# Moving the two halves of x by 192 bytes and the weight units by 256 in SBUF, in a two-layer hybrid trunk on one core

## The chip, the cores and the metric

The kernel runs on one core of a Trainium2 chip. The metric is device time in microseconds (us) for one execution of the whole program; lower is better. The core has TensorE (PE in the profile, its weight loads PEld), VectorE (DVE), ScalarE (ACT), GpSimd (POOL) and SyncE (SP), which here only issues DMAs.

## The reference

Two layers, each of three residual blocks with a LayerNorm behind each: a SwiGLU block, a mixer, a second SwiGLU block. x is 512 tokens by 1024 features in float32; the inner width of a SwiGLU block is 2816.

```python
for l in range(DEPTH):                       # DEPTH = 2
    x = layer_norm(ALPHA * x + 0.5 * swiglu_ffn(x, ffn1_w_gu[l], ffn1_w_down[l]), ...)
    x = layer_norm(ALPHA * x + hybrid_mixer(x, w_in[l], w_out[l], ...), ...)
    x = layer_norm(ALPHA * x + 0.5 * swiglu_ffn(x, ffn2_w_gu[l], ffn2_w_down[l]), ...)

def swiglu_ffn(x, w_gu, w_down):
    a, u = jnp.split(x @ w_gu, 2, axis=-1)
    return (jax.nn.silu(a) * u) @ w_down
```

The mixer projects x once, runs windowed softmax attention on one group of heads and chunked retention on the other, and projects the two outputs back.

## The kernel before, in words

**Every product in three.** A float32 operand is split into a high part, rounded to the matmul format fp32r, and a low part, the rest. `split` (L168, L169) does it: ACT casts the high part, DVE subtracts it for the low one. `mm3` (L183 to L185) then issues three matmuls for one product: high by high, the stationary high with the moving low, the stationary low with the moving high. Its argument `a` is the stationary operand, loaded into the array by a weight load ahead of the matmul; `b` is the moving operand. In the profile's rows a matmul stands as `ps<-moving,stationary`: `ps<-xh,uh` streams xh past the weights uh.

**The tiles that matter here.** `xh` and `xl` are the high and low parts of the transposed x, 8 blocks of 128 features by 512 tokens, 16384 bytes a partition each. Weights arrive by DMA in `raw`, are split into `uh` and `ul` ("units", 4096 bytes a partition, six buffers each), and are handed out by `Weights.get`. `Th` and `Tl` are the split differences of x's quarters, made once in each SwiGLU block by `sums_of_x`.

**A SwiGLU block**, of which there are four. The gate and up products come in 11 steps of 256 columns; steps 2 to 10 are done by `glu7`, a seven-product scheme on 2 by 2 blocks. There the units are stationary and 256 tokens are streamed; of its 14 products of 12 matmuls, 6 stream a quarter of x (`xb`) and 8 stream a difference (`tb`). Steps 0 and 1 use `projs`, with 256 or 512 tokens of x streamed. The down projection that follows (`seventh`, `down`) turns the roles round: a slice of x's buffers, which by then hold splits of the inner activations, is stationary, and a unit is streamed, 512 columns wide. The residual, LayerNorm (`norm`) and the transposes back into xh and xl close the block.

**The mixer** streams x past stationary units for queries and keys (`emit_T`, 256 tokens wide for five of the units, and `projs`, 512 wide), and streams units past stationary x for values, gates and the output (`proj_tok`, `half`).

**Order.** The recording layer keeps the program order on TensorE and for the splits (`keep_in_program_order`); a pool's buffer is reused when its last reader is done. Pools are laid out in SBUF one behind the other in the order in which they are opened: `base`, `rawp`, `unit`, `small`, then the pools of the stage.

**Where the tiles lie.** From the built program, in bytes from the start of each partition: 2048 of DMA scratch, four constants of 32 each, `ident` (512), `mhalf` (32), and then xh at 2720, which is 160 modulo 256. xl, Y and raw follow in multiples of 256, so the units begin at 68256, also 160 modulo 256, with all twelve buffers alike. `small` takes 960 bytes, and the pools of a SwiGLU block begin at 118368. Th lies at 179808 and Tl at 196192, both 96 modulo 256. Each block and slice of these tiles that a matmul reads starts a multiple of 512 bytes behind its tile's start, so the remainder modulo 256 is the same for all of a tile's matmuls.

Of the kernel before, what the change touches and what calls it, by code (L numbers as in the profile page):

```python
# [7 lines left out]
F32 = mybir.dt.float32  # L8
# [10 lines left out]
P = 128  # L19
# [27 lines left out]
class Weights:  # L47


    def __init__(self, T, items):  # L50
        self.T, self.items = T, items
        self.emitted = self.taken = self.out = 0
        self.ready = []
        self.raws = {}
        self.last = {raw: i for i, (raw, _, _, _) in enumerate(items)}
# [44 lines left out]
class Trunk:  # L100
    def __init__(self, tc, ctx):
        self.tc, self.nc = tc, tc.nc
        self.n = 0
        self.now = 0
        self.pin = True
        self.tasks = []
        self.later = []
        self.pace = None
        self.halves = 2
        nc = self.nc  # L110
        self.base = ctx.enter_context(tc.tile_pool(name="base", bufs=1))
        self.rawp = ctx.enter_context(tc.tile_pool(name="rawp", bufs=2))
        self.unit = ctx.enter_context(tc.tile_pool(name="unit", bufs=UBUFS))
        self.small = ctx.enter_context(tc.tile_pool(name="small", bufs=3))
        self.psum = ctx.enter_context(tc.tile_pool(name="psum", bufs=8, space=PSUM))
        self.ident = self.base.tile([P, P], F32, name="ident")
        make_identity(nc, self.ident)
        self.mhalf = self.base.tile([P, 8], F32, name="mhalf")
        nc.vector.memset(self.mhalf, -0.5)
        self.xh = self.base.tile([P, KC, SEQ], F32R, name="xh")  # L120
        self.xl = self.base.tile([P, KC, SEQ], F32R, name="xl")
        self.Y = self.base.tile([P, NT, D], F32, name="Y")
# [370 lines left out]
    def norm(self, t, halves, gb, out=None, delay=4, scale=(ALPHA, ALPHA)):  # L493
        nc = self.nc
        g, b = gb
        y = self.Y[:, t, :]
        st = self.small.tile([P, 2, 6], F32, tag="st", name=self.nm("st"))
        for h in range(2):
            hs = slice(h * 512, (h + 1) * 512)
            nc.vector.scalar_tensor_tensor(out=y[:, hs], in0=y[:, hs], scalar=scale[h], in1=halves[h],  # L500
                                           op0=ALU.mult, op1=ALU.add)
            nc.vector.bn_stats(out=st[:, h, :], in_=y[:, hs])
        mv = self.small.tile([P, 2], F32, tag="mv", name=self.nm("mv"))
        nc.vector.bn_aggr(out=mv, in_=st)
        ve = self.small.tile([P, 1], F32, tag="ve", name=self.nm("ve"))
        nc.vector.tensor_scalar_add(ve, mv[:, 1:2], LN_EPS)
        rs = self.small.tile([P, 1], F32, tag="rs", name=self.nm("rs"))
        nc.gpsimd.tensor_tensor(out=rs, in0=ve, in1=self.mhalf[:, 0:1], op=ALU.pow)
        nc.vector.scalar_tensor_tensor(out=y, in0=y, scalar=mv[:, 0:1], in1=g, op0=ALU.subtract, op1=ALU.mult)
        parts = [slice(0, D)] if out is None else [slice(0, 512), slice(512, D)]  # L510
        for hs in parts:
            nc.vector.scalar_tensor_tensor(out=y[:, hs], in0=y[:, hs], scalar=rs, in1=b[:, hs],
                                           op0=ALU.mult, op1=ALU.add)
            if out is not None:
                nc.sync.dma_start(out[t * P : (t + 1) * P, hs], y[:, hs])
        if out is None:
            self.pend.append(self.spawn(self.y_to_xT(t), delay))
# [670 lines left out]
```

## Time and profile before

| | |
|---|---|
| Median of 3 runs | 1766.88 us (1766.7 to 1767.4) |
| Span of the profiled execution, first to last instruction | 1765.1 us |
| Median less that span | 1.8 us |
| TensorE busy | 99% of the span, 11930 matmuls |
| Weight loads busy | 91%, 11930 loads |
| DVE / ACT / POOL busy | 80% / 53% / 10% |

The page gives the span of the profiled execution; that execution's own device time is not listed apart, so the 1.8 us between span and median stand for what lies around the span. Matmuls overlap in the array, so the sum of their durations is more than the span; what one matmul costs when they stand in a row is the distance from its start to the next one's start, called its pitch below. "Granted clock" is the share of TensorE's clock that the throttle let through.

### The profile page before, as it was taken

The numbers are of one execution on the slowest core, as the hardware profiler recorded it, in microseconds if no ns is written. First come the engines' busy times: TensorE is split into PE (matmuls) and PEld (weight loads), VectorE is DVE, ScalarE is ACT, GpSimd is POOL, SyncE is SP. The second block draws the span as 40 slices with busy tenths as digits, with TensorE's granted clock in tenths as the row PEclk, the third lists the DMA queues.
The fourth block names the chain that finished last, engine by engine and source line by source line (L and its number), as shares of the span: only waits on it lengthen the run. The fifth ranks groups of instructions, "written<-read, shape, count | busy, mean of one in ns | idle before, by whom it ended". The sixth has DMA issues, their size and how long they took to land.

```text
span 1765.1 us, 29166 instructions
## 1 busy us (share of the span) xinstructions
PE 1752.7 (99%) x11930; PEld 1600.5 (91%) x11930; DVE 1414.9 (80%) x1975; ACT 928.1 (53%) x1456; POOL 182.9 (10%) x152
## 2 busy tenths in 40 slices
PE   9999999999999999999999999999999999999998
PEld 9999988887789999998899999889877899999886
DVE  7888888856767888878888888888567587888887
ACT  5455556378712455555535555554795234555561
POOL 0000022111111000014000000311011110000131
PEclk9999999999999999999999999999999999999999
DMA  6234389422222243369423334982233122334891
GB/s 191 97 96 133 131 202 199 131 85 88 73 79 72 74 137 102 97 208 214 140 68 99 121 96 147 211 203 91 85 95 96 48 95 97 97 96 132 211 218 48
DMA packets 163765, 216.34 MB, mean 123 GB/s; under 512 B 5168, under 2 KB 116528, under 8 KB 163632
## 3 DMA queue, kind: packets, MB, share of 16 engines
q1 hardware_dynamic: 141872, 172.55, 30.5%
q0 software_dynamic: 21760, 41.95, 13.1%
q8 instruction: 93, 1.52, 0.3%
q14 instruction: 40, 0.33, 0.1%
HBM read 212.38 MB, written 2.10 MB: 122 GB/s over the span
## 4 chain that ended last, share of the span: by engine, by line
PE 90%; issue 6%; DMA 1%; DVE 1%; POOL 1%; ACT 0%; SPq 0%; POOLq 0%; DVEq 0%
PE ps L183 29%; PE ps L185 29%; PE ps L184 29%; PE ps L476 1%; DMA raw<-in_ffn_w_gu_dram 1%; POOL sw L959 1%; PE ps L1067 1%; PE ps L1015 0%; PE ps L1029 0%; PE ps L1063 0%; PE ps L1050 0%; DMA retS<-c_retS_dram 0%; ACT sw L957 0%; DVE ul L169 0%; PE ps L1007 0%
## 5 line engine op out<-in xcount | busy, mean ns | idle before, releaser
L183 PE MATMUL ps<-xh,uh 128*128 128x256 f32 (+1 forms) x1616 | 482.2, 298 | 0.0
L185 PE MATMUL ps<-xh,ul 128*128 128x256 f32 (+1 forms) x1616 | 479.3, 297 | 1.0 <-DVE ul L169 0.9
L184 PE MATMUL ps<-xl,uh 128*128 128x256 f32 (+1 forms) x1616 | 478.5, 296 | 0.3 <-DVE xl L169 0.3
L168 ACT CAST uh<-raw 128x1024 fp32r<-128x1024 f32 (+1 forms) x274 | 237.1, 886 | 245.6 <-PE ps L184 140.1
L169 DVE TENSOR_TENSOR ul<-raw,uh 128x1024 fp32r<-128x1024 f32 (+1 forms) x274 | 273.3, 1013 | 62.2 <-ACT uh L168 61.6
L183 PE MATMUL ps<-Th,uh 128*128 128x256 f32 x1152 | 319.1, 277 | 0.0
L184 PE MATMUL ps<-Tl,uh 128*128 128x256 f32 x1152 | 318.7, 277 | 0.0
L185 PE MATMUL ps<-Th,ul 128*128 128x256 f32 x1152 | 318.3, 276 | 0.0
L185 PEld LDWEIGHTS ps<-xh,ul 128*128 128x128 f32 x1616 | 307.9, 191 | 10.1 <-DVE ul L169 1.6
L183 PEld LDWEIGHTS ps<-xh,uh 128*128 128x128 f32 x1616 | 307.9, 191 | 9.7 <-issue 1.6
L184 PEld LDWEIGHTS ps<-xl,uh 128*128 128x128 f32 x1616 | 308.0, 191 | 7.9 <-DVE xl L169 0.5
L183 PE MATMUL ps<-uh,xh 128*128 128x512 f32 x720 | 283.4, 394 | 0.5 <-ACT xh L168 0.5
L185 PE MATMUL ps<-uh,xl 128*128 128x512 f32 x720 | 280.8, 390 | 0.0
L184 PE MATMUL ps<-ul,xh 128*128 128x512 f32 x720 | 280.3, 389 | 0.0
L168 ACT CAST uh<-S 128x1024 fp32r<-128x1024 f32 x144 | 151.1, 1049 | 149.0 <-PE ps L184 145.2
L169 DVE TENSOR_TENSOR ul<-S,uh 128x1024 fp32r<-128x1024 f32 x144 | 175.9, 1222 | 60.1 <-ACT uh L168 59.5
L184 PEld LDWEIGHTS ps<-Tl,uh 128*128 128x128 f32 x1152 | 216.7, 188 | 0.0
L183 PEld LDWEIGHTS ps<-Th,uh 128*128 128x128 f32 x1152 | 216.6, 188 | 0.0
L185 PEld LDWEIGHTS ps<-Th,ul 128*128 128x128 f32 x1152 | 216.4, 188 | 0.0
L389 POOL DMA_DIRECT2D R<-in_ffn_w_down_dram x80 | 97.1, 1217 | 1020.7 <-DVE ul L169 930.0
L169 DVE TENSOR_TENSOR ul<-R,uh 128x1024 fp32r<-128x1024 f32 x120 | 145.1, 1221 | 25.8 <-ACT uh L168 25.7
L183 PEld LDWEIGHTS ps<-uh,xh 128*128 128x128 f32 x720 | 135.2, 188 | 30.1 <-issue 1.6
(143 smaller groups left out, 2362.4 us busy)
## 6 DMA issues: line engine op xcount, KB each, us to landing
raw<-in_ffn_w_gu_dram SPq DMA_DIRECT2D x86, 1024.0 KB, 5.5
R<-in_ffn_w_down_dram POOLq DMA_DIRECT2D x80, 512.0 KB, 7.6
raw<-in_w_in_dram SPq DMA_DIRECT2D x18, 1024.0 KB, 5.2
R<-in_ffn_w_down_dram SPq DMA_DIRECT2D x16, 1024.0 KB, 6.3
raw<-in_ffn_w_down_dram SPq DMA_DIRECT2D x12, 1024.0 KB, 7.2
R<-in_ffn_w_down_dram SPq DMA_DIRECT2D x8, 512.0 KB, 4.3
raw<-in_w_in_dram SPq DMA_DIRECT2D x8, 512.0 KB, 6.1
raw<-in_w_out_dram SPq DMA_DIRECT2D x8, 512.0 KB, 6.4
```

What stands on the lines that cost most here:

```text
L168: a = self.nc.scalar.copy(hi, src)
L169: b = self.low = self.nc.vector.tensor_sub(lo, src, hi.bitcast(F32))
L183: keep(mm(out, ah, bh, start=start, stop=False, **kw))
L184: keep(mm(out, ah, bl, start=False, stop=False, **kw))
L185: keep(mm(out, al, bh, start=False, stop=stop, **kw))
L389: self.nc.gpsimd.dma_start(src, rows(i, j, g * 2, 2), accum_op=ALU.add))
L476: nc.tensor.transpose(b[:, c * P : (c + 1) * P], src[:, c * P : (c + 1) * P], self.ident)
L959: nc.gpsimd.tensor_mul(sw[:, :n], sw[:, :n], S)
L1067: ins = nc.tensor.matmul(ob[:, o0 : o0 + HD], ST[h][:, n, :], vr[:, n, p * P + h * HD : p * P + (h + 1) * HD], start=n == 0, stop=n == 0 o ...
```

## The change

It moves tiles in SBUF. Three statistics tiles of 64 bytes (`st0` to `st2`) are allocated in `base` ahead of xh, in place of the rotating `st` of `small`; that moves xh, xl, Y and raw up by 192 bytes. A new pool `near` of 64 bytes stands between raw and the units, which moves the units up by 256. `ve` becomes a third column of `mv`, and a pad of 32 bytes (`behind`) is put into `small`; `small` is 256 bytes shorter by all this, so every pool behind it stays where it was. The two pads are written once, by two GpSimd memsets.

| tile | before | modulo 256 | after | modulo 256 |
|---|---|---|---|---|
| xh | 2720 | 160 | 2912 | 96 |
| xl | 19104 | 160 | 19296 | 96 |
| raw, first of two | 51872 | 160 | 52064 | 96 |
| uh, first of six | 68256 | 160 | 68512 | 160 |
| ul, first of six | 92832 | 160 | 93088 | 160 |
| Th | 179808 | 96 | 179808 | 96 |
| Tl | 196192 | 96 | 196192 | 96 |

```diff
         self.rawp = ctx.enter_context(tc.tile_pool(name="rawp", bufs=2))
+        self.near = ctx.enter_context(tc.tile_pool(name="near", bufs=1))
+        nc.gpsimd.memset(self.near.tile([P, 16], F32, name="apart"), 0.0)
         self.unit = ctx.enter_context(tc.tile_pool(name="unit", bufs=UBUFS))
...
+        nc.gpsimd.memset(self.small.tile([P, 8], F32, tag="behind", name="behind", bufs=1), 0.0)
...
+        self.stats = [self.base.tile([P, 2, 8], F32, name=f"st{i}") for i in range(3)]
+        self.norms = 0
         self.xh = self.base.tile([P, KC, SEQ], F32R, name="xh")
...
-        st = self.small.tile([P, 2, 6], F32, tag="st", name=self.nm("st"))
+        st = self.stats[self.norms % 3][:, :, :6]
+        self.norms += 1
...
-        mv = self.small.tile([P, 2], F32, tag="mv", name=self.nm("mv"))
-        nc.vector.bn_aggr(out=mv, in_=st)
-        ve = self.small.tile([P, 1], F32, tag="ve", name=self.nm("ve"))
+        mv = self.small.tile([P, 3], F32, tag="mv", name=self.nm("mv"))
+        ve = mv[:, 2:3]
+        nc.vector.bn_aggr(out=mv[:, :2], in_=st)
```

The order of instructions on TensorE, ACT, DVE and SP is what it was, with the same waits between the same instructions. On GpSimd two memsets are added at the start of the program. Its first rows before (`ident` is the identity matrix that TensorE's first matmuls use):

```order
L1174 MEMSET const-uint8-127 128x1
L1184 UNCONDITIONAL_BRANCH
masks.py:197 MEMSET ident 128x128
masks.py:199 ISA
masks.py:199 AFFINE_SELECT ident<-ident 128x128
```

And now:

```order
L1180 MEMSET const-uint8-127 128x1
L1190 UNCONDITIONAL_BRANCH
L114 MEMSET apart 128x16
L118 MEMSET behind 128x8
masks.py:197 MEMSET ident 128x128
masks.py:199 ISA
masks.py:199 AFFINE_SELECT ident<-ident 128x128
```

The two memsets stand ahead of the two instructions that make `ident`; nothing else has moved.

## The prediction

> **What bounds the kernel now.** I read the page's busy times and clock first, then the waits of TensorE, then the groups of instructions kept apart by shape, and last the order of time inside two stages.
>
> ```profile
> PE 1752.7 (99%) x11930; PEld 1600.5 (91%) x11930; DVE 1414.9 (80%) x1975; ACT 928.1 (53%) x1456; POOL 182.9 (10%) x152
> PEclk9999999999999999999999999999999999999999
> PE 90%; issue 6%; DMA 1%; DVE 1%; POOL 1%; ACT 0%; SPq 0%; POOLq 0%; DVEq 0%
> PE ps L468 <- POOL ident masks.py:199: 1.4, 1, 1.4
> PE ps L185 <- DVE ul L169: 0.9, 2, 0.7
> ```
>
> The first row is busy time by engine, the second the granted clock in 40 slices (nine tenths or more all along), the third the shares of the chain that ended last. The last two are the longest waits of TensorE in the whole program: 1.4 us at the start and 0.9 us. TensorE is neither waiting nor throttled, so time changes only where its matmuls follow each other closer or less close. The rows by shape hold nearly all of it (names are moving, stationary; then count, busy us, mean ns of one):
>
> ```profile
> L183 PE MATMUL ps<-xh,uh 128*128 128x256 f32 x1408 | 398.5, 283 | 0.0
> L185 PE MATMUL ps<-xh,ul 128*128 128x256 f32 x1408 | 398.1, 283 | 1.0 <-DVE ul L169 0.9
> L184 PE MATMUL ps<-xl,uh 128*128 128x256 f32 x1408 | 397.3, 282 | 0.3 <-DVE xl L169 0.3
> L183 PE MATMUL ps<-Th,uh 128*128 128x256 f32 x1152 | 319.1, 277 | 0.0
> L184 PE MATMUL ps<-Tl,uh 128*128 128x256 f32 x1152 | 318.7, 277 | 0.0
> L185 PE MATMUL ps<-Th,ul 128*128 128x256 f32 x1152 | 318.3, 276 | 0.0
> L183 PE MATMUL ps<-uh,xh 128*128 128x512 f32 x720 | 283.4, 394 | 0.5 <-ACT xh L168 0.5
> L184 PE MATMUL ps<-ul,xh 128*128 128x512 f32 x720 | 280.3, 389 | 0.0
> L183 PE MATMUL ps<-xh,uh 128*128 128x512 f32 x208 | 83.6, 402 | 0.0
> L183 PE MATMUL ps<-uh,hr 128*128 128x512 f32 x64 | 25.2, 394 | 0.0
> ```
>
> Streaming 256 columns of x takes 6 ns longer than streaming 256 columns of a difference: same shape, type, weights and clock. Durations overlap in the array, so I look at starts, in three runs of matmuls without a wait:
>
> ```profile
> 100.00 0.28 PE L183 MATMUL ps<-xh,uh 128*128 128x256 f32 x1
> ...
> 101.80 0.28 PE L183 MATMUL ps<-xh,uh 128*128 128x256 f32 x1
> ...
> 102.16 0.29 PE L183 MATMUL ps<-Th,uh 128*128 128x256 f32 x1
> ...
> 102.52 0.28 PE L183 MATMUL ps<-Th,uh 128*128 128x256 f32 x1
> ...
> 103.08 0.28 PE L185 MATMUL ps<-Th,ul 128*128 128x256 f32 x1
> ...
> 108.52 0.28 PE L185 MATMUL ps<-Th,ul 128*128 128x256 f32 x1
> ...
> 250.07 0.39 PE L183 MATMUL ps<-uh,xh 128*128 128x512 f32 x1
> ...
> 252.79 0.39 PE L183 MATMUL ps<-uh,xh 128*128 128x512 f32 x1
> ...
> L185 PE MATMUL ps<-Th,ul 128*128 128x256 f32 x13 | 3.6, 276 | 0.0
> L183 PE MATMUL ps<-xh,uh 128*128 128x256 f32 x4 | 1.1, 283 | 0.0
> ```
>
> From 100.00 to 101.80 are 15 matmuls on x: 120.0 ns each. From 103.08 to 108.52 are 48 on a difference: 113.3 ns. From 250.07 to 252.79 are 12 of the 512-wide ones: 226.7 ns, twice 113.3. The last two rows are the mean durations in such steady stretches, 103 to 107 us and 45.0 to 46.2 us. Duration less pitch is 163 ns in all three (283 less 120, 276 less 113.3, 389 less 226.7), so a mean duration tells a mean pitch.
>
> Now the addresses. A matmul on x has moving and stationary operand at the same remainder modulo 256 (160 and 160); one on a difference has 96 and 160. That is the only thing I find that tells the two groups apart in their operands, besides rival 1's. All 512-wide groups have equal remainders: uh and xh 160, and the last units of the down projection with `hr`, which lie in the stage's own pool, 96 and 96.
>
> **The change, part by part.**
>
> *x streamed 256 wide, 3 x 1408 = 4224 matmuls.* They get exactly the remainders of the differences, 96 and 160. Mean duration of the three x rows: 1193.9 us / 4224 = 282.65 ns. Of the three difference rows: 956.1 / 3456 = 276.65; in their steady stretch 276. If x comes to the steady 276, the gain is 6.65 ns x 4224 = 28.1 us; if only to the mean, 6.0 x 4224 = 25.3 us. All of it lies on TensorE's path, which waits for nothing.
>
> *The differences themselves, 3456 matmuls.* Their mean is 0.65 ns above their steady value; in the order of time the first three behind a product on x (102.16 to 102.52) still have x's 120 ns. With both kinds alike the changeover should go: 0.65 x 3456 = 2.2 us. Bounds 0 and 2.2; I take 2.2, since within a run of differences the products change without it.
>
> *512 wide, unit streamed past x, 3 x 720 = 2160 matmuls (and 3 x 208 = 624 with x streamed past a unit).* In the first, remainders go from 160 and 160 to 160 and 96, a pair no row shows: x is now loaded 64 below the stream, not 64 above. I bound a matmul's price by -6.65 ns (as in the 256-wide ones) and +13 ns (the slowest 512-wide group, 402, against 389). I take 0. These rows say why, the weight loads with their mean ns, and the first 256-wide matmuls behind a run of 512-wide ones:
>
> ```profile
> L184 PEld LDWEIGHTS ps<-xl,uh 128*128 128x128 f32 x1616 | 308.0, 191 | 7.9 <-DVE xl L169 0.5
> L184 PEld LDWEIGHTS ps<-Tl,uh 128*128 128x128 f32 x1152 | 216.7, 188 | 0.0
> L184 PEld LDWEIGHTS ps<-ul,xh 128*128 128x128 f32 x720 | 135.3, 188 | 26.9
> ...
> 57.14 0.39 PE L185 MATMUL ps<-xh,ul 128*128 128x512 f32 x1
> 57.37 0.28 PE L183 MATMUL ps<-xh,uh 128*128 128x256 f32 x1
> 57.48 0.28 PE L184 MATMUL ps<-xl,uh 128*128 128x256 f32 x1
> 57.60 0.28 PE L185 MATMUL ps<-xh,ul 128*128 128x256 f32 x1
> 57.72 0.28 PE L183 MATMUL ps<-xh,uh 128*128 128x256 f32 x1
> ```
>
> Loads beside 256-wide x take 191 ns (a row that holds the 208 of its 512-wide matmuls too), loads beside differences 188, and loads beside 512-wide matmuls 188 although their remainders are equal. Behind the 512-wide run the first matmul on x still has a pitch of 0.11 us, and only then 0.12. So I read the 6.7 ns as a load that comes late where one load has to fit into one 113 ns matmul; beside 227 ns of streaming it has room, at any remainder.
>
> *The feeding engines.* A faster TensorE asks for weights sooner. In the first `glu7` stage (the columns are PE, PEld, DVE and ACT busy, with counts):
>
> ```profile
> 61.00:231.00 170.00, 170.00 (x1466) 170.00 (x1465) 145.46 (x214) 94.77 (x143) 0.00 (x0) 1.00 0.36 115
> ACT uh L168 <- PE ps L184: 59.8, 59, 1.5
> ```
>
> A `glu7` step has 168 matmuls, 72 of them on x, so the 1466 of this stretch are 8.7 steps; it shrinks by 8.7 x 72 x 6.65 ns = 4.2 us and by 0.5 us for its differences, to 165.3, and DVE is then busy 88% of it. The second row is a wait in the same stretch: the casts wait 59 times for TensorE to give a unit back, 59.8 us in all. What is late next is that wait, which only gets shorter. Price 0; up to half of the gain if the splits should fall behind.
>
> *raw at another remainder.* Casts out of raw (160) and out of S (96) compare so:
>
> ```profile
> L168 ACT CAST uh<-raw 128x1024 fp32r<-128x1024 f32 x166 | 173.7, 1052 | 185.0 <-PE ps L184 84.0 <-PE ps L185 47.1 <-DMA raw<-in_ffn_w_gu_dram 31.1
> L168 ACT CAST uh<-S 128x1024 fp32r<-128x1024 f32 x144 | 151.1, 1049 | 149.0 <-PE ps L184 145.2 <-DVE ul L169 3.7
> ```
>
> 3 ns in 166 casts, off the path: 0.
>
> *Two memsets on GpSimd, ahead of `ident`.* The nearest rows are the constants' memsets and the first transposes:
>
> ```profile
> 0.24 0.10 POOL L1174 MEMSET const-float32-0.0<- 128x1 f32 x1 [0.24 <-issue]
> 0.27 0.10 POOL L1174 MEMSET const-float32-1.0<- 128x1 f32 x1
> ...
> 5.83 0.66 PE L476 MATMUL ps<-ident,Y 128*128 128x128 f32 x4 [0.30 <-DMA Y<-in_x_dram]
> ```
>
> They start 0.03 us apart and last 0.10, so `ident`, and with it TensorE's first matmul, comes 0.06 to 0.20 us later. At 5.83 TensorE stands idle for 0.30 us until the second tile of x lands; that covers it. Without the cover it would cost 0.2 us at most. The statistics tiles and `ve` keep engine, order and waits; their DVE rows lie off TensorE's path except in the last 10 us. Price 0, at most 0.1 us either way.
>
> *Sum.* 1765.1 - 28.1 - 2.2 = 1734.8 us of span; with the 1.8 us by which the median lies above the span, 1736.6. I say 1737.
>
> **Rivals.**
>
> 1. *The remainder is not the cause.* The two groups differ in two more ways: x and the units lie below byte 117,500 of the partition and the differences above 179,800, and x's blocks are 2048 bytes apart, those of the differences 1024. Every 512-wide group has both operands in the same one of these regions as well, so the rows do not tell far addresses from remainders. If one of these is the cause, nothing moves: 1767 us. Against it: the units' buffers lie from 68256 to 117,408, those of uh below those of ul, and x is as slow with the one as with the other (283 and 283 in the rows of L183 and L185), so distance as such does nothing; a border between 117,500 and 179,800 is not excluded. [...] 15 in 100.
>
> 2. *Every matmul pays for equal remainders, the 512-wide ones too.* 226.7 would then be 220. For it: no row shows a 512-wide matmul at unequal remainders, so nothing excludes that each holds the same 6.65 ns. Against it: the loads of 188 ns and the first pitch of 0.11. Gain 2784 x 6.65 = 18.5 us more: 1718 us. 10 in 100.
>
> 3. *The other side of zero costs.* In the 2160 matmuls with x stationary the load now runs 64 below the stream. At +6.65 ns each that is +14.4 us: 1751 us (4 in 100). At the row's bound of 13 ns, +28.1 us: 1764.7, no change (2 in 100). It is slower than before from (30.3 + 3.5) / 2160 = 15.7 ns on; the place would be the down projections, 389 ns growing to over 405 (4 in 100).
>
> 4. *The period is 512, not 256.* Units move by 256 and the differences do not, so their distance goes from 64 to 320. If that made the 3456 differences as slow as x is now, +23.0 us, while x gains 28.1 and the changeovers' 2.2 is lost: 1762 us. 4 in 100.
>
> 5. *The splits fall behind* and half is lost: 1752 us. 5 in 100.
>
> **The numbers.** My forecast has 56 in 100 and 1737 us; its own range is 1734 to 1742: from 25.3 us of gain to 30.3 and 2.1 more for the rounding of the steady 276 (0.5 ns x 4224). 0.2% (3.5 us) is about what a measurement of this kernel can tell from no change. Faster by more: 56 + rival 2's 10, rival 3's first 4, rival 5's 5 and rival 4's 4 = 79. Within: 15 + 2 = 17. Slower: 4. The range reaches up to rival 1, which is likelier than rival 2 and leaves that one out: 1732 (the own range and 2 us for the 512-wide rows' unknown price) to 1768 holds the forecast, rivals 1, 4 and 5 and most of 3, 86 in 100.
>
> **What would show it.** Right: the rows of x streamed 256 wide at 276 ns and a pitch of 113.3, their loads at 188, the differences' rows at 276, the 512-wide rows unchanged, and each `glu7` stage some 4.5 us shorter. Rival 1 leaves 283; rivals 2 and 3 show in the 512-wide rows with x stationary, 382 or 396 and more; rival 4 in the rows of Th and Tl; rival 5 in waits of TensorE on ACT or DVE. The forecast is wrong above all if the low address bits are not what tells x from its differences.

## The result and the profile after

The changed kernel took 1751.5 us (median of 4 executions: 1750.87, 1751.06, 1751.94, 1757.87) against 1767.07 us before, a ratio of 0.992 with a 95% interval of 0.9904 to 0.9936. In a second measurement it took 1750.96 us (1750.7 to 1752.3), ratio 0.9912 (0.9897 to 0.9927). The gain is 15.6 us in the first and 15.5 in the second (before took 1766.45 there); 30 were forecast. The profiled execution of the first measurement is the one of 1757.87 us (span 1756.1), that of the second one of 1750.9 (span 1749.1). Both are used below, since the difference between them turned out to be the main finding: of the eight executions of the new kernel seven took 1751 to 1752 us and one some 6.7 us more.

TensorE is as full as before. These are its busy times and the longest of its waits in the execution of 1757.87 us (line waited for, releaser, us, times, longest); its other waits come to 1.4 us together:

```profile
PE 1744.9 (99%) x11930; PEld 1585.7 (90%) x11930; DVE 1414.6 (81%) x1975; ACT 927.3 (53%) x1456; POOL 181.6 (10%) x154
PE ps L473 <- POOL ident masks.py:199: 1.5, 1, 1.5
```

So again only the rows of matmuls can move the time. (Line numbers are 5 higher than before: L183 to L185 are now L188 to L190.) The groups by shape, first of the execution of 1757.87 us:

```profile
L188 PE MATMUL ps<-xh,uh 128*128 128x256 f32 x1408 | 392.7, 279 | 0.0
L190 PE MATMUL ps<-xh,ul 128*128 128x256 f32 x1408 | 392.1, 279 | 0.5 <-DVE ul L174 0.3
L189 PE MATMUL ps<-xl,uh 128*128 128x256 f32 x1408 | 391.9, 278 | 0.4 <-DVE xl L174 0.4
L188 PE MATMUL ps<-Th,uh 128*128 128x256 f32 x1152 | 319.4, 277 | 0.0
L188 PE MATMUL ps<-uh,xh 128*128 128x512 f32 x720 | 285.2, 396 | 0.5 <-ACT xh L173 0.5
L189 PE MATMUL ps<-ul,xh 128*128 128x512 f32 x720 | 282.6, 392 | 0.0
L190 PE MATMUL ps<-uh,xl 128*128 128x512 f32 x720 | 281.0, 390 | 0.0
L188 PE MATMUL ps<-xh,uh 128*128 128x512 f32 x208 | 84.5, 406 | 0.0
L190 PE MATMUL ps<-xh,ul 128*128 128x512 f32 x208 | 82.1, 395 | 0.0
```

And the rows that differ in the one of 1750.9 us; its 512-wide rows are the same to 0.1 us:

```profile
L188 PE MATMUL ps<-xh,uh 128*128 128x256 f32 x1408 | 391.5, 278 | 0.0
L190 PE MATMUL ps<-xh,ul 128*128 128x256 f32 x1408 | 390.9, 278 | 0.9 <-DVE ul L174 0.7
L189 PE MATMUL ps<-xl,uh 128*128 128x256 f32 x1408 | 390.8, 278 | 0.4 <-DVE xl L174 0.4
L188 PE MATMUL ps<-Th,uh 128*128 128x256 f32 x1152 | 318.0, 276 | 0.0
```

x streamed 256 wide came down from 283 to 278 or 279 ns, not to 276; the 512-wide rows went up, from 394, 389 and 390 to 396, 392 and 390 with x stationary, and from 402 and 391 to 406 and 395 with x streamed. Since a duration is pitch plus some 163 ns (283 less 120 and 276 less 113.3 before), differences of the busy sums add up to the change of the span. In us against before (1765.1):

| group | 1750.9 execution | 1757.87 execution | forecast |
|---|---|---|---|
| x streamed 256 wide, 4224 | 1173.2 - 1193.9 = -20.7 | 1176.7 - 1193.9 = -17.2 | -28.1 |
| differences, 3456 | 954.0 - 956.1 = -2.1 | 958.2 - 956.1 = +2.1 | -2.2 |
| 512 wide, x stationary, 2160 | 848.8 - 844.5 = +4.3 | +4.3 | 0 |
| 512 wide, x streamed, 624 | 248.8 - 246.0 = +2.8 | +2.7 | 0 |
| sum | -15.7 | -8.1 | -30.3 |
| span | 1749.1 - 1765.1 = -16.0 | 1756.1 - 1765.1 = -9.0 | -30.3 |

(The last 512-wide sums use the third row of that group too: 82.1 us after and 81.2 before, 390 ns then.) The rows hold the whole change to within 1 us. Two questions are left: why the 512-wide rows cost 7 us, and why the 256-wide rows of two executions of one program differ by 7.7.

The second is seen when matmuls are counted in 160 us of each of the four `glu7` stages. Before, the first stage (start to end, length, TensorE busy with its count; then clock, DMA share, GB/s); the other three show 1379 or 1380:

```profile
65.00:225.00 160.00, 160.00 (x1380) 1.00 0.36 116
```

The changed kernel in the execution of 1757.87 us, first and second stage (the other two count 1414 as well), and behind it the first stage of the one of 1750.9, whose four stages all count 1414:

```profile
65.00:225.00 160.00, 160.00 (x1361) 1.00 0.35 113
605.00:765.00 160.00, 160.00 (x1414) 1.00 0.36 113
```
```profile
65.00:225.00 160.00, 160.00 (x1414) 1.00 0.37 122
```

160 us over 1414 are 113.2 ns, the steady pitch that the forecast put there; over 1380 they are 115.9, before's mix of 120 and 113.3; over 1361 they are 117.6 (slightly low, since matmuls that stick out at the ends of the stretch are counted too). With the same remainders, the same clock and no wait, a whole stage ran some 4.5 ns a matmul slower, longer even than before: from its first matmul to the one behind its last it took 178.1 us instead of 171.4, 6.7 us more; before took 175.7. The order of time at the stage's beginning, in the execution of 1757.87 us and then of 1750.9:

```profile
56.83 0.28 PE L188 MATMUL ps<-xh,uh 128*128 128x256 f32 x1
...
57.89 0.28 PE L188 MATMUL ps<-xh,uh 128*128 128x256 f32 x1
...
103.12 0.28 PE L188 MATMUL ps<-Th,uh 128*128 128x256 f32 x1
...
108.77 0.28 PE L188 MATMUL ps<-Th,uh 128*128 128x256 f32 x1
```
```profile
56.65 0.28 PE L188 MATMUL ps<-xh,uh 128*128 128x256 f32 x1
...
57.68 0.28 PE L188 MATMUL ps<-xh,uh 128*128 128x256 f32 x1
...
102.89 0.28 PE L188 MATMUL ps<-Th,uh 128*128 128x256 f32 x1
...
108.67 0.28 PE L188 MATMUL ps<-Th,uh 128*128 128x256 f32 x1
```

The same 512-wide matmuls stand ahead of the stage in both. From 56.83 to 57.89 are 9 steps of 117.8 ns, from 56.65 to 57.68 nine that average 114. 46 us later it is 48 steps of 117.7 and 51 of 113.3. The row goes on as it began.

The stages don't hold all of x's shortfall. 2592 of the 4224 matmuls on x are in the `glu7` stages; the other 1632 are in steps 0 and 1 and in the mixers, in rows of 24 to 192. The durations of single matmuls in the traces, added up, split x's 1193.9 us of before into 731.0 in the stages and 463.0 outside, and the 1173.2 of the 1750.9 execution into 715.5 and 457.8. At 6.65 ns each, the forecast had 17.2 us in the stages and 10.9 outside; it got 15.5 and 5.2. Outside, 1141 of the 1632 still last 280 to 283 ns in this execution (1236 in the other). One such row, from 890 to 910 us:

```profile
L190 PE MATMUL ps<-xh,ul 128*128 128x256 f32 x57 | 16.0, 281 | 0.0
```

### The profile page after: what moved, and what is told of

Same layout as the page of the kernel before. It is cut to its first block, busy times and chain, and to the rows that moved or that the text cites. A ratio compares the mean times of both kernels' runs of the same rounds, so it can differ in the third digit from the quotient of the medians.

```text
span 1756.1 us, 29168 instructions
## 1 busy us (share of the span) xinstructions
PE 1744.9 (99%) x11930; PEld 1585.7 (90%) x11930; DVE 1414.6 (81%) x1975; ACT 927.3 (53%) x1456; POOL 181.6 (10%) x154
## 4 chain that ended last, share of the span: by engine, by line
PE 97%; DVE 1%; DMA 1%; ACT 0%; SPq 0%; POOLq 0%; issue 0%; DVEq 0%; ACTq 0%
PE ps L188 31%; PE ps L189 30%; PE ps L190 30%; DMA raw<-in_ffn_w_gu_dram 1%; PE ps L481 1%; PE ps L1021 1%; PE ps L986 1%; PE ps L1073 1%; PE ps L1013 1%; PE ps L1035 1%; DVE ul L174 0%; PE ps L1069 0%; PE ps L1056 0%; PE ps L1046 0%; ACT uh L173 0%; DVE xl L174 0%
## 5 line engine op out<-in xcount | busy, mean ns | idle before, releaser
L188 PE MATMUL ps<-xh,uh 128*128 128x256 f32 (+1 forms) x1616 | 477.2, 295 | 0.0
L190 PE MATMUL ps<-xh,ul 128*128 128x256 f32 (+1 forms) x1616 | 474.3, 293 | 0.5 <-DVE ul L174 0.3
L188 PE MATMUL ps<-Th,uh 128*128 128x256 f32 x1152 | 319.4, 277 | 0.0
L190 PE MATMUL ps<-Th,ul 128*128 128x256 f32 x1152 | 319.4, 277 | 0.0
L188 PEld LDWEIGHTS ps<-xh,uh 128*128 128x128 f32 x1616 | 304.0, 188 | 10.5 <-issue 1.6
L190 PEld LDWEIGHTS ps<-xh,ul 128*128 128x128 f32 x1616 | 303.5, 188 | 10.5 <-DVE ul L174 1.1
L188 PE MATMUL ps<-uh,xh 128*128 128x512 f32 x720 | 285.2, 396 | 0.5 <-ACT xh L173 0.5
L190 PE MATMUL ps<-uh,xl 128*128 128x512 f32 x720 | 281.0, 390 | 0.0
L190 PEld LDWEIGHTS ps<-Th,ul 128*128 128x128 f32 x1152 | 216.3, 188 | 0.0
L188 PEld LDWEIGHTS ps<-Th,uh 128*128 128x128 f32 x1152 | 216.2, 188 | 0.0
L188 PEld LDWEIGHTS ps<-uh,xh 128*128 128x128 f32 x720 | 135.3, 188 | 32.2 <-issue 1.6
```

The source lines that it names most:

```text
L188: keep(mm(out, ah, bh, start=start, stop=False, **kw))
L190: keep(mm(out, al, bh, start=False, stop=stop, **kw))
```

## The experiments

**Do the pads and the moved statistics do anything?** x and the units both at 160, the rest of the change as it is:

```diff
-        self.near = ctx.enter_context(tc.tile_pool(name="near", bufs=1))
-        nc.gpsimd.memset(self.near.tile([P, 16], F32, name="apart"), 0.0)
...
+        nc.gpsimd.memset(self.base.tile([P, 16], F32, name="apart"), 0.0)
         self.xh = self.base.tile([P, KC, SEQ], F32R, name="xh")
```

> All of the change, but the 64 bytes of the pad between raw and the units stand ahead of xh: x at 160 and the units at 160 modulo 256, both 256 bytes above their old places. Theory 1: the matmuls are those of before, x 256 wide 283 ns, differences 277, 512 wide 389 to 394: 1767 us. Rival (the distance counts modulo 512, or the statistics tiles and pads do something themselves): the differences' rows or the total differ from before by more than 0.2%.

1766.41 us, ratio 0.9997 (0.9986 to 1.0009), with before's durations:

```profile
L187 PE MATMUL ps<-xh,uh 128*128 128x256 f32 x1408 | 398.5, 283 | 0.0
L187 PE MATMUL ps<-Th,uh 128*128 128x256 f32 x1152 | 319.1, 277 | 0.0
```

All of the effect comes from the remainders of x. The units lie 256 bytes further up here and the differences stay put, yet these keep 277 ns: a distance of 320 serves them as 64 did, so the period is 256 here, not 512.

**Is it the remainder, or where the tile lies?** Th and Tl moved by 64 bytes to the units' remainder, x as in the change:

```diff
+            nc.gpsimd.memset(gp.tile([P, 16], F32, name=self.nm("shift")), 0.0)
```

> The change, and 64 bytes ahead of Th, so that Th and Tl are at 160 as the units are, while x stays at 96. Theory 1: the two kinds trade places: differences 283 ns (pitch 120), x 276 in its steady stretches since each row of differences breaks a slow cadence; 512-wide rows as in the changed kernel. Against the changed kernel's sum that is +20 us for 3456 matmuls at 120 instead of 114.4 and about -10 us for x: 1760 to 1766 us. Rival (far address or block distance tells the kinds apart): differences stay at 276 to 277.

1775.16 us, ratio 1.0045 (1.0025 to 1.0064):

```profile
L188 PE MATMUL ps<-xh,uh 128*128 128x256 f32 x1408 | 392.8, 279 | 0.0
L188 PE MATMUL ps<-Th,uh 128*128 128x256 f32 x1152 | 325.3, 282 | 0.0
```

64 bytes put the differences at 282 ns, about x's old duration, in the same place 100 KB from the units. In the `glu7` stages x did come to 276, here from 95.5 to 99.5 us:

```profile
L188 PE MATMUL ps<-xh,uh 128*128 128x256 f32 x13 | 3.6, 276 | 0.0
```

In each stage x stands in 27 rows, the first at its head and 26 behind rows of differences at distance 0, and each of them has 276 or 277 ns from its seventh matmul on. The mean of 279 comes from the 1632 outside, which average 280.8 ns. That is why the total came out above my 1760 to 1766 us: the 10 us that I expected of x came to 0.9 (1175.8 us against the changed kernel's 1176.7). The bookkeeping by rows holds (differences +19.3, x -18.1, 512 wide +7.0: +8.2; span 1773.0 - 1765.1 = +7.9).

**Is any unequal remainder good?** x at 32, so 128 away from the units, by a larger pad and one statistics tile less:

```diff
-        nc.gpsimd.memset(self.near.tile([P, 16], F32, name="apart"), 0.0)
+        nc.gpsimd.memset(self.near.tile([P, 32], F32, name="apart"), 0.0)
...
-        self.stats = [self.base.tile([P, 2, 8], F32, name=f"st{i}") for i in range(3)]
+        self.stats = [self.base.tile([P, 2, 8], F32, name=f"st{i}") for i in range(2)]
```

> x at 32 modulo 256, 128 below the units; differences stay 64 below, two statistics tiles instead of three. Theory 1: a third distance gives x its own cadence, between 113 and 118 ns for 256 columns, and since x's and the differences' distances are unlike, each change between them breaks a slow cadence, so the differences return to 276; 512-wide matmuls at 227 to 234 ns. Total 1740 to 1760 us. Rival (only 64 bytes below does it): x at 120 ns, 1767 us or more.

1777.78 us, ratio 1.0058 (1.0036 to 1.0081):

```profile
L188 PE MATMUL ps<-xh,uh 128*128 128x256 f32 x1408 | 397.6, 282 | 0.0
L188 PE MATMUL ps<-uh,xh 128*128 128x512 f32 x720 | 286.8, 398 | 0.5 <-ACT xh L173 0.5
```

x gains 1 ns and the 512-wide row loses 4 (394 before); the time misses my 1740 to 1760 us and lies on the rival's side. So it is not inequality that helps 256 columns, and the 512-wide row fares best at 0 so far: 394 there, 396 at +64 in the changed kernel, 398 at 128.

**The map.** A kernel that computes no layer: 48 matmuls in a row per pair of width and distance (streamed start less loaded start), on a core that does nothing else; for each, once behind 24 at distance 0 and once from idle.

```python
m0 = i % 4 * N + d // 4
keep(fn(mm, o[:, :N], U[:, i % 8, :], M[:, m0 : m0 + N], start=i == 0, stop=i == n - 1))
```

> Matmuls alone on the core, no layer is computed: 48 in a row for each distance (streamed less loaded start address) of 0 to 448 bytes and for widths of 256 and 512, once behind 24 matmuls at distance 0 and once from idle. Theory 1 (the remainder modulo 256 sets the cadence, and away from 0 a row can fall into either of two cadences, by how it begins): 256 wide, distance 0 gives a duration of 283 ns, distance 192 (64 below) 276 behind distance 0 and 276 or 281 from idle; 448 reads like 192, 256 and 320 like 0 and 64; 512 wide, 389 at 0, 396 at 192, 391 at 64. Rival (the distance to the other tiles or the other engines' traffic makes the two cadences, not the pair of addresses): every 256-wide block shows one value, 276 or less, at all distances, and 512 wide 389 everywhere.

The blocks behind distance 0: 256 wide at 0, 64, 96, 192 (that is, -64) and 448, then 512 wide at 0, 64 and 192. The second number behind the bar is the mean duration:

```profile
L15 PE MATMUL ps<-M,U 128*128 128x256 f32 x48 | 5.9, 283 | 0.0
L21 PE MATMUL ps<-M,U 128*128 128x256 f32 x48 | 5.8, 279 | 0.0
L23 PE MATMUL ps<-M,U 128*128 128x256 f32 x48 | 5.9, 282 | 0.0
L29 PE MATMUL ps<-M,U 128*128 128x256 f32 x48 | 5.6, 276 | 0.0
L37 PE MATMUL ps<-M,U 128*128 128x256 f32 x48 | 5.6, 276 | 0.0
L39 PE MATMUL ps<-M,U 128*128 128x512 f32 x48 | 11.0, 389 | 0.0
L45 PE MATMUL ps<-M,U 128*128 128x512 f32 x48 | 11.2, 392 | 0.0
L53 PE MATMUL ps<-M,U 128*128 128x512 f32 x48 | 11.4, 394 | 0.0
```

256 columns have their minimum at -64 (276; all other distances tried lie from 279 to 283), and 448 repeats 192. For 512 columns it is the other way round: 0 is best (389), +64 costs 3 ns and -64 five. Taken at the steady end of each block, the pitches are 120.0, 117.8 and 113.3 ns for 256 columns at 0, +64 and -64, and 226.7, 228.9 and 233.3 for 512. The down projections went from 0 to +64: 2.2 ns x 2160 = 4.8 us, where their rows show 4.3. The 512-wide products with x streamed went from 0 to -64: 6.6 x 624 = 4.1, where theirs show 2.8. That answers the first question.

**What chooses between 113 and 118 ns?** Again no layer: 48 matmuls of 256 columns at -64, each time behind another entry; three repeats.

```python
row(fn, b, 256, 448, 48, u, m)      # behind one of 21 entries
```

> Matmuls alone, no layer is computed: 48 in a row of 256 columns streamed 64 bytes below the loaded operand, three times behind each of 21 entries (idle, 1 to 12 matmuls at distance 0, 24 to 26 of 512 columns at distances 0, 64 below and 64 above, transposes, a wait for fresh weights or a fresh stream in mid-row, and some of these with 1 to 12 matmuls at distance 0 in between). Theory 1 (the way in sets the cadence, and it then stays): each entry gives one of two values, 276 ns (pitch 113.3) or 281 (117.8), the same in its three repeats; from idle and behind 12 matmuls at distance 0 276, behind 512 columns at distance 0 281, and 12 matmuls at distance 0 put between turn that into 276. Rival (other engines' traffic or the chip's state makes the slow cadence): all entries 276, since nothing else runs here.

From above: behind 2 and behind 3 matmuls of 256 columns at distance 0, behind 24 and behind 25 of 512 columns at -64, behind 24 of 512 at 0, and behind these with 3 of 256 at 0 put in between (144 matmuls each, all three repeats together; with 12 put in between it is 276 too):

```profile
L18 PE MATMUL ps<-M,U 128*128 128x256 f32 x144 | 16.8, 276 | 0.0
L19 PE MATMUL ps<-M,U 128*128 128x256 f32 x144 | 17.4, 281 | 0.0
L22 PE MATMUL ps<-M,U 128*128 128x256 f32 x144 | 16.8, 276 | 0.0
L23 PE MATMUL ps<-M,U 128*128 128x256 f32 x144 | 17.4, 281 | 0.0
L21 PE MATMUL ps<-M,U 128*128 128x256 f32 x144 | 17.4, 281 | 0.0
L33 PE MATMUL ps<-M,U 128*128 128x256 f32 x144 | 16.9, 276 | 0.0
```

At -64 a row of 256-wide matmuls shows two cadences here, 276 and 281 ns, and keeps the one that it comes to in its first few matmuls; one matmul more ahead of it changed which (276 behind two at distance 0, 281 behind three). Both came up without the layer's work on the other engines. Most entries gave the same in all three repeats; four transposes, and nine matmuls followed by fresh weights, gave now one, now the other (means of 280 ns).

**Does breaking the row bring the fast cadence into the kernel?** Twelve matmuls of a unit on itself (distance 0, their sums thrown away) at the head of each `glu7` stage, and the unaltered changed kernel beside it:

```diff
+                    if fp == SEVEN[0] and m == 0:
+                        for i in range(RESET):                       # RESET = 12
+                            tc.keep_in_program_order(
+                                nc.tensor.matmul(A[0][:, :256], u[0][:, i % KC, :],
+                                                 u[0].rearrange("p k c -> p (k c)")[:, i % 3 * 256 : i % 3 * 256 + 256],
+                                                 start=i == 0, stop=i == RESET - 1))
                     product(A[m], u, 0, xb(0, 0))
```

> The change, and 12 matmuls of 256 columns at distance 0 (a unit streamed past itself; their sums are overwritten) at the start of each of the four glu7 stages. They cost 4 x 12 x 120 ns = 5.8 us. Theory 1: all four glu7 stages then run at 113.3 ns throughout, also where the changed kernel's profile has 117.8: 1512 x 4.5 ns = 6.7 us less than its profiled execution, and 1757 us whenever the changed kernel would have had 1751. Rival: the stage's cadence is the same as without them, fast in some stages and slow in others.

> The changed kernel once more. Theory 1: the time falls on steps 6.7 us apart, by how many of the four glu7 stages are entered in the slow cadence: 1751 us with none, 1758 with one; the other rows (512 wide 389 to 406 ns, differences 276 in a fast stage) as in its first profile. Rival (drift or the chip's state): times spread evenly, and the first stage has a cadence between the two.

1756.92 us (1756.52 to 1757.01), ratio 0.9944 (0.9928 to 0.9961), all four stages at 1414 or 1415 matmuls in 160 us, and executions within 0.5 us of each other. The 48 extra matmuls cost 5.8 us, and the unaltered kernel took 1750.96 beside it, with all four stages fast that time: insurance at nearly the price of the damage.

Three instead of twelve, at the first product on x of each mixer and each SwiGLU block but the first:

```diff
+                if settle:
+                    self.settle(a, au[0])
...
+                if kind == "k" and t0 == 0:
+                    self.settle(b_, u)
```

> The change, and three matmuls of 256 columns at distance 0 ahead of the first matmul on x in each mixer and in each SwiGLU block but the first: 5 x 0.36 = 1.8 us of added work. Theory 1: the stretches of 240 to 288 matmuls behind them, at 117.8 ns in the changed kernel's profiles, run at 113.3: 4 x 250 x 4.45 ns = 4.4 us less, so 1748 to 1750 us. Rival (the cadence has its cause in the stretch itself, its waits or the other engines): they stay at 117.8, and the time is 1753 us.

1757.42 us (1749.12 to 1764.09, 6 executions), ratio 0.9942 (0.9922 to 0.9962). The row that starts right behind the three matmuls is fast in all five places of the profiled execution (1751.13 us); in both profiled executions of the changed kernel it is fast in two of the five. Here from 878 to 888 us, where the 1750.9 execution has 281:

```profile
L191 PE MATMUL ps<-xh,ul 128*128 128x256 f32 x31 | 8.6, 276 | 0.0
```

But it did not last: of the rows that follow behind a break some are fast and some slow, so the 1632 matmuls outside the stages took 455.7 us instead of 457.8, 2.1 us less and not 4.4, at a price of 1.8. The six times lie in groups near 1750, 1757 and 1764, one step of 6.7 us apart, as if the `glu7` stages, which have no matmuls put ahead of them here, fell either way as before; all four are fast in the one execution that was profiled.

**Can both widths have their best remainder?** One tile with 64 bytes to spare; x lies at 96 for the gate and up products and at 160 for the down projections and the mixers:

```diff
+        self.X = self.base.tile([P, 2 * KC * SEQ + 16], F32R, name="X")
+        self.look(BELOW)
...
+            self.look(down_at)
```

> A version meant to keep the gain and give back the loss: xh and xl lie in one tile with 64 spare bytes, and each stage picks its start. While a SwiGLU block streams x past units, x lies at 96 (64 below the units); in the down projections that are followed by a mixer or by nothing, and in the mixers up to their output projection, it lies at 160 as the units do. The pad between raw and units is gone. Theory 1 (the remainders of the two operands set the cadence, equal ones being best for 512 columns): the 512-wide rows there return to 227 ns, some 1670 matmuls with x loaded at 2.2 ns less and 432 with x streamed at 6.7 ns less, against 480 matmuls of 256 columns in the mixers that go to 120: about 5 us less than the change, 1746 us. Rival (the 512-wide rows are slower for the pads, not for the pair of addresses): 1751 us, or more by the mixers' 480 matmuls.

1754.72 us (7 executions, 1752.22 to 1769.54), ratio 0.9944 (0.9922 to 0.9966); 1746 was forecast. The profiled execution is the lowest, 1752.22. In it the 512-wide rows lie 3.2 us (x stationary) and 1.5 us (x streamed) below those of the change, where 1670 x 2.2 ns = 3.7 and 432 x 6.7 ns = 2.9 were expected, and in the last `glu7` stage the slow cadence took the gain away. What the longer executions ran, one of them longer than those before the change, no trace shows. One 512-wide row, and the last stage:

```profile
L194 PE MATMUL ps<-uh,X 128*128 128x512 f32 x720 | 283.9, 394 | 0.5 <-ACT X L179 0.5
1476.00:1636.00 160.00, 160.00 (x1360) 1.00 0.37 120
```

Settling matmuls were added to it in three ways: three at the start of the SwiGLU blocks but the first, three at the head of each `glu7` stage, and twelve there.

```diff
+                if settle:                           # first of the three kernels
+                    self.settle(a, au[0])
...
+                    if fp == SEVEN[0] and m == 0:    # the others: as above, RESET = 3 and 12
```

> Both: each stage picks x's start, and three matmuls at distance 0 ahead of the SwiGLU blocks but the first. Theory 1: 1744 to 1746 us, the lowest of all. Rival: not below the version without the three matmuls, 1746 to 1748 us.

> As the run with x at 96 before 256-wide use and at 160 before 512-wide use (its profiled execution: 1752.2 us, span 1750.4, last glu7 stage in the slower cadence), and three extra products of a unit on itself, distance 0, at the head of each glu7 stage, their sums thrown away. Theory (the cadence of a row of matmuls at -64 bytes is chosen where the row begins, and three at distance 0 ahead of it choose 113.3 ns): all four glu7 stages at 113.3 ns, 1752.2 - 6.7 for the last stage + 12 extra matmuls x 0.12 = 1.4 us: 1747 us, and no run a stage (6.7 us) above it. Rival (the cadence is drawn anew by something else, such as what the other engines do at that moment): one or more glu7 stages at 117.8 as without them, 1753 to 1760 us, in steps of 6.7.

> The same with twelve instead of three. Theory: 48 extra x 0.12 = 5.8 us, 1752.2 - 6.7 + 5.8 = 1751 us, all four glu7 stages at 113.3 ns, and steadier than 1 us from run to run. If three are too few and twelve enough, this one is faster than the run with three in its slow runs only. Rival: glu7 stages at 117.8 here too, 1758 us and more.

They took 1754.96 us (ratio 0.9925, 0.9913 to 0.9936), 1756.61 (0.9946, 0.9932 to 0.996) and 1753.93 (0.9925, 0.9913 to 0.9938). The first two stages of the second, then the first of the third and a stretch near its start, and two rows in order of time out of that stretch:

```profile
65.00:225.00 160.00, 160.00 (x1360) 1.00 0.35 113
605.00:765.00 160.00, 160.00 (x1414) 1.00 0.36 116
```
```profile
65.00:225.00 160.00, 160.00 (x1414) 1.00 0.36 117
24.00:36.00 12.00, 11.24 (x83) 0.86 0.28 91
```
```profile
26.84 0.41 PE L195 MATMUL ps<-X,uh 128*128 128x256 f32 x1
...
28.98 0.41 PE L196 MATMUL ps<-X,uh 128*128 128x256 f32 x1
```

The first was forecast at 1744 to 1746 us and missed it: in its profiled execution (1754.96 us) the three rows right behind the three matmuls are fast, but the last `glu7` stage is slow (1361). Three at the stage's head left two stages of four slow (the first, above, and the third, with 1361), so my theory that three are enough fell; the stand-alone rows had 281 ns behind three alone as well. With twelve all four count 1414, but the profiled execution took 1755.99 us instead of the 1751 I gave it. It lost some 4 us in its first 45 (its 512-wide products of the first block begin at 48.4 us, those of the run with three at 44.4): a wait of 2.0 us for a unit's cast, and then a granted clock of 0.86 over 12 us, which the other executions profiled of this kernel and its variants (1.00) don't show at that place; ten steps from 26.84 to 28.98 are 214 ns each. Its executions scatter from 1751.81 to 1755.99, not within the 1 us that I expected. No version's median beat the change itself.

## Why the prediction was right or wrong

**What bounds the kernel** was right: TensorE hardly waits (2.9 us in all) and is not throttled (granted clock 0.999) after the change, and the sums of its rows give the change to within 1 us.

**x streamed 256 wide, -28.1 us: right in cause, too large.** The rows show -20.7 and -17.2. The remainder is the cause: the run with x back at 160 shows 283 again, and moving the differences to 160 made them slow (282 ns). What failed is the step from the steady 276 ns of the differences to 276 for all of x. 276 was one of two cadences. In the 1750.9 execution, with four fast stages, the miss lies almost all outside the stages: 5.7 us, as 1141 of the 1632 matmuls there kept the other cadence, 281 ns. In the stages it is 1.7 us, since x had 282.0 ns there before and not the 282.65 of its mean. The execution of 1757.87 us has a slow stage on top. That the slow cadence never showed in the `glu7` stages before fits the order of the program: there a product on x, at distance 0, came between the differences every few products, 12 or more matmuls of it. The change gave x and its differences one remainder, so that nothing breaks the row any more, and a stage that starts at 117.8 ns stays there, as the first one of the 1757.87 execution did (178.1 us). The four kernels in which x and the differences have unlike distances (before, both at 160, the differences at 160, x at 32) bear this out: in their 16 stages 428 rows at -64 stand behind such a break, and each has 276 or 277 ns from its seventh matmul on. What draws a stage's cadence at its start is less well shown: twelve matmuls at distance 0 went with the fast cadence in all 8 stages profiled, against 19 of 24 in the six profiled executions with both kinds at -64 and none or three in place of the twelve. At that rate eight of eight would come by chance about one time in seven.

**The differences, -2.2 us: right where all four stages run fast** (-2.1), and turned round to +2.1 by one slow stage. The changeover at 120 ns did go.

**512 wide, 0: the term that was mis-sized.** It measured +4.3 us for the 2160 with x stationary and +2.8 for the 624 with x streamed, both inside the bounds of -6.65 and +13 ns a matmul. I took a load beside 227 ns of streaming to have room at any remainder, from loads of 188 ns and one first pitch of 0.11 us. But all 512-wide rows of before stood at distance 0, the best one for that width in the map (389 ns behind distance 0, against 392 to 396 at the others), so they could not show the cost; that a load has room there was my estimate, and no run shows it. This load is still 188 ns after the change, where its matmul costs 3 ns more, so the load's duration was no measure of it:

```profile
L189 PEld LDWEIGHTS ps<-ul,xh 128*128 128x128 f32 x720 | 135.4, 188 | 26.9
```

**The feeding engines, raw, the memsets, 0: right.** TensorE's longest wait is 1.5 us, at the start (1.4 before), and the casts out of raw take 1049 ns (1052 before).

**The rivals.** The first, that the remainder is not the cause, is refuted by the differences at 160 (282 ns instead of 277) and by the map, where one shape takes 276 to 283 ns by the distance of its two operands alone. The second, a gain for 512-wide matmuls, is refuted by sign. The third, a cost on the other side of zero, is the one that came true, at a third of its lower price (2.0 ns from the rows, 2.2 from the map, not 6.65), and the same kind of cost in the 624 that I had not given a rival. The fourth, a period of 512, is refuted by the map and by the differences' 277 ns with the units moved. The fifth did not occur.

**The range and the chances.** 1751.5 lies inside 1732 to 1768 and is faster by more than 0.2%, but outside the 1734 to 1742 that I gave the forecast itself. That it also meets rival 3's 1751 is luck: that rival had all of the loss in the 2160 matmuls. Of the 14.6 us by which the 1750.9 execution falls short of the forecast sum, 7.4 are x's and 7.1 the 512-wide rows'.

**What stays open**: what in the machine makes 0 best for 512 columns and -64 for 256, and what picks the cadence. The stand-alone runs show that what stands ahead of a row decides and that a single matmul shifts it (276 ns behind two at distance 0, 281 behind three); the mechanism was not seen.

## What to carry to other kernels

Where TensorE's rows of one shape differ by a few ns (here 283 and 277), compare the start addresses of the streamed and the loaded operand modulo 256 bytes, and measure each width by itself before a tile is moved: a tile used at two widths may gain in one and lose in the other (here -20.7 us at 256 columns and +7.1 at 512). A steady stretch in a trace shows one value that a row took, not that it takes no other (here 276 ns before the change, 276 or 281 after it); count matmuls per stage in several executions. If executions of a kernel that hardly waits fall on steps (here of 6.7 us), look for a stage whose whole row runs at another pitch.

## What the runs showed of the hardware

- For the fp32r matmuls of the map the pitch depends on the streamed start less the loaded start modulo 256 bytes: behind distance 0, 113.3 to 120.0 ns for 256 columns (mean durations 276 at -64, the best, and 283 and 282 at 0 and 96, the worst), 226.7 to 234 for 512 (389 at 0, the best, and 392 to 396 at the others). One row of 512 had two values as well: at -16 (240 in the map) 233.3 ns behind distance 0 and 226.6 from idle (mean durations 396 and 390).
- At -64, a row of 256 columns showed two cadences, 113.3 and 117.8 ns. It kept its own over a stage of 1512 matmuls (171.4 or 178.1 us), across changes of weights, operands and PSUM targets, and 24 or 25 matmuls of 512 columns at -64 ahead of it were enough of a difference to choose (276 and 281 ns). Rows in the `glu7` stages that stand behind 12 or more matmuls at distance 0 or 128 came to 276 or 277 ns, the pitch of 113.3, each time (428 rows).
- One execution, with twelve matmuls at the head of each stage and x at two places, showed a granted clock of 0.86 from 24 to 36 us (1.00 there in the others). Waits of 2.0 and 0.8 us with two matmuls between stand ahead of it, and 15 steps between matmuls of 256 columns, from 25.99 to 29.19 us, average 213 ns; from 29.34 on they are 0.12 us again. What lowered the clock was not shown.
